# Gate/up products of a hybrid decoder block with tokens on partitions, three groups of tiles by Strassen's seven block products, and weight splits by whole pages

## Chip, cores, metric

One core of one Trainium2 chip runs the whole block in one launch. The metric is the device time in microseconds, as the median of several runs; less is better. A profile of one further execution gives the trace.

## What is computed

One decoder layer on 256 tokens of width 1024, all in fp32: a mixer (eight block-sparse MoBA heads and four differential heads, merged by two gates, one output projection), then a feed-forward part of width 2816. The change is in the feed-forward, but for the splits of weights, which serve every product.

```python
D_MODEL = 1024; SEQ = 256
D_FF = -(-8 * D_MODEL // (3 * 256)) * 256        # 2816
def reference(x, ..., w_gate, w_up, w_down, norm_ffn_post_g):
    ...
        merged = (jax.nn.sigmoid(ga) * (ya @ w_branch_a[l])
                  + jax.nn.sigmoid(gb) * (yb @ w_branch_b[l]))
        x = x + rms_norm(merged @ w_out[l], norm_mix_post_g[l])
        h = rms_norm(x, norm_ffn_pre_g[l])
        f = (jax.nn.silu(h @ w_gate[l]) * (h @ w_up[l])) @ w_down[l]
        x = x + rms_norm(f, norm_ffn_post_g[l])
    return x
```

## The kernel before

**Products.** Each operand is split exactly into two float32r parts, hi + lo, and each fp32 product is three matmuls: hi by hi, hi by lo, lo by hi (`mm3`, L227 to L229). Weights come raw from HBM through one ring of `RB` = 7 tiles of 128x1024 (512 KB), in one fixed order, all from SP's queue (`load_raws`, L191): a load waits until the tile seven before it has been split. ScalarE copies the raw half of 128x512 to hi (L209, `whi`), VectorE takes raw minus hi as lo (L212, `wlo`); the hi and lo tiles are rings of `WB` = 5.

**Order.** The work is a list of slots, each about 12 products of N=256. `run` walks through it, and before each slot it issues the splits that the next four slots need. PE and SP keep that order; ScalarE's, VectorE's and GpSimd's queues are ordered by the framework's scheduler, but for two stretches written by hand.

**Input projection and merge.** `group_T` makes q and k with columns on partitions, 4 banks `acc` of 512 columns each; VectorE takes a bank out by L446 (q). After the attention, `ab_slots` makes both branches; their products with the gates are added on GpSimd (L694, `mg`) and split into `mTh`, `mTl`, which `out_part` multiplies by w_out.

**Feed-forward.** The first four column tiles of gate and up (`NAT` = 4) have tokens on partitions: `nat`, with `h2h`/`h2l` stationary and 512 weight columns moving. Their result is turned by eight transposes (`nat_T`, L929). The other 18 tiles, f = 4 to 21, go through `gu_slots(f)`: a weight block of 128x128 is stationary, `h2h`/`h2l` of 128x256 moving, 8 k blocks x 3 x 2 (gate, up) = 48 matmuls of N=256 into one bank `s`. `ff_act` takes it out: times the column factor R2 (L882), silu, times up (L885), split into `fth`, `ftl`. R2 is made by `r2` (L909), products of ones by diagonal matrices `dg`. Behind tile f come the down terms of the tile before, `z_slots("d", ..)`: 15 matmuls, nine of N=512 and six of N=256, into three banks `acc` and one `pv`. The last four down terms are arranged by pieces (`z_tail`), and then come the norm, the residual and the output.

```python
    for f in range(NAT, NFF):
        slots += gu_slots(f)
        if f == NAT:
            slots[-2]["post"] = [nat_T]
        for i in downs(f):
            slots += z_slots("d", i, f_of, NFF - 1)
```

Of the kernel before, what the change touches and what calls it, by code (L numbers as in the profile page):

```python
# [64 lines left out]
def tile_hybrid_block(  # L65
# [37 lines left out]
    raws, gran, halves, extra, place = [], {}, [], [], {}  # L103

    def raw_of(w, r0, nr, c0, ncol):
        raws.append(dict(view=w[0, r0:r0 + nr * P, c0:c0 + ncol].rearrange("(a p) c -> p a c", p=P),
                         a=nr, c=ncol, uses=0, tile=None))
        return raws[-1]
# [897 lines left out]
```

## Time and profile before

| | |
|---|---|
| runs, us | 385.74, 385.76, 386.1; median 385.76 |
| span of the profiled execution, us | 383.0 |
| granted TensorE clock, mean | 0.995 |
| PE / VectorE / ScalarE / GpSimd busy, us | 375.3 / 270.9 / 221.6 / 40.2 |
| moved by DMA | 67.72 MB, mean 177 GB/s |

The profiled execution has no time of its own beside its span: the span runs from its first to its last instruction, and the device time of the runs has the launch and the end around it. PE is TensorE's matmul row, PEld its weight loads, DVE is VectorE, ACT ScalarE, POOL GpSimd, SP the queue that issues the loads. Busy times of PE overlap, since a matmul is still draining when the next one starts; what a matmul costs in a stream is read from start to start. A wait is shown as idle time before an instruction, with the instruction or load that released it.

### The profile page before, as it was taken

The numbers are of one execution on the slowest core, as the hardware profiler recorded it, in microseconds if no ns is written. First come the engines' busy times: TensorE is split into PE (matmuls) and PEld (weight loads), VectorE is DVE, ScalarE is ACT, GpSimd is POOL, SyncE is SP. The second block draws the span as 40 slices with busy tenths as digits, with TensorE's granted clock in tenths as the row PEclk, the third lists the DMA queues.
The fourth block names the chain that finished last, engine by engine and source line by source line (L and its number), as shares of the span: only waits on it lengthen the run. The fifth ranks groups of instructions, "written<-read, shape, count | busy, mean of one in ns | idle before, by whom it ended". The sixth has DMA issues, their size and how long they took to land.

```text
span 383.0 us, 7077 instructions
## 1 busy us (share of the span) xinstructions
PE 375.3 (98%) x2648; PEld 349.3 (91%) x2648; DVE 270.9 (71%) x596; ACT 221.6 (58%) x492; POOL 40.2 (11%) x59
## 2 busy tenths in 40 slices
PE   8999999999999999999999999999999999999993
PEld 5799989999999999998888998999999999999983
DVE  3799887989978769798768755655656566567524
ACT  4965675778565866555578544545445454456321
POOL 0199400000001002122100000000000000000000
PEclk9999999999999999999999999999999999999997
DMA  7989656263555436487118872755729274563003
GB/s 211 377 267 357 178 162 173 67 193 104 186 164 165 166 111 221 167 273 213 61 56 272 256 236 71 265 158 174 251 86 307 75 273 134 196 222 110 2 0 111
DMA packets 43813, 67.72 MB, mean 177 GB/s; under 512 B 2801, under 2 KB 27394, under 8 KB 43778
## 3 DMA queue, kind: packets, MB, share of 16 engines
q1 hardware_dynamic: 43778, 67.26, 53.8%
q8 instruction: 21, 0.34, 0.4%
q14 instruction: 14, 0.11, 0.1%
HBM read 66.20 MB, written 1.05 MB: 176 GB/s over the span
## 4 chain that ended last, share of the span: by engine, by line
PE 93%; DVE 2%; issue 2%; DMA 1%; SPq 0%; ACT 0%; POOLq 0%; POOL 0%; DVEq 0%; ACTq 0%
PE acc L227 14%; PE acc L229 13%; PE acc L228 13%; PE s L229 12%; PE s L228 12%; PE s L227 12%; PE acc L506 5%; PE pv L228 2%; PE pv L229 2%; PE pv L227 2%; DVE wlo L212 1%; DMA wraw<-in_w_in_dram 1%; PE t L228 1%; PE t L229 1%; PE t L227 1%
## 5 line engine op out<-in xcount | busy, mean ns | idle before, releaser
L212 DVE TENSOR_TENSOR wlo<-wraw,whi 128x512 fp32r<-128x512 f32 x234 | 157.7, 712 | 51.3 <-ACT whi L209 50.9
L209 ACT ACTIVATE whi<-wraw 128x512 fp32r<-128x512 f32 x233 | 133.9, 624 | 89.8 <-issue 42.1
L229 PE MATMUL s<-h2h,wlo 128*128 128x256 f32 x288 | 81.0, 281 | 0.0
L227 PE MATMUL s<-h2h,whi 128*128 128x256 f32 x288 | 80.9, 281 | 0.0
L228 PE MATMUL s<-h2l,whi 128*128 128x256 f32 x288 | 80.9, 281 | 0.0
L227 PE MATMUL acc<-hTh,whi 128*128 128x256 f32 x256 | 73.1, 286 | 0.4 <-DVE q L446 0.4
L229 PE MATMUL acc<-hTh,wlo 128*128 128x256 f32 x256 | 71.8, 281 | 0.0
L228 PE MATMUL acc<-hTl,whi 128*128 128x256 f32 x256 | 71.8, 281 | 0.0
L228 PEld LDWEIGHTS s<-h2l,whi 128*128 128x128 f32 x288 | 54.4, 189 | 0.0
L227 PEld LDWEIGHTS s<-h2h,whi 128*128 128x128 f32 x288 | 54.4, 189 | 0.0
L229 PEld LDWEIGHTS s<-h2h,wlo 128*128 128x128 f32 x288 | 54.2, 188 | 0.0
L227 PEld LDWEIGHTS acc<-hTh,whi 128*128 128x128 f32 x256 | 48.3, 189 | 0.7 <-DVE q L446 0.6
L228 PEld LDWEIGHTS acc<-hTl,whi 128*128 128x128 f32 x256 | 48.3, 189 | 0.0
L229 PEld LDWEIGHTS acc<-hTh,wlo 128*128 128x128 f32 x256 | 48.2, 188 | 0.0
L227 PE MATMUL acc<-whi,fth 128*128 128x512 f32 (+1 forms) x80 | 29.2, 365 | 0.0
L229 PE MATMUL acc<-whi,ftl 128*128 128x512 f32 (+1 forms) x80 | 29.1, 364 | 0.0
L228 PE MATMUL acc<-wlo,fth 128*128 128x512 f32 (+1 forms) x80 | 29.0, 362 | 0.0
L772 POOL TENSOR_TENSOR rs_r<-rs_e,mhalf 128x1 f32<-128x1 f32 x4 | 2.2, 552 | 190.3 <-DVE rs_e L771 190.3
L882 DVE TENSOR_TENSOR gs<-s,R 128x256 f32<-128x256 f32 x18 | 7.7, 425 | 16.4 <-PE s L229 16.4
L551 ACT ACTIVATE e<-e,nmx 128x256 f32<-128x256 f32 (+1 forms) x32 | 14.3, 447 | 5.8 <-DVE nmx L548 5.4
L229 PEld LDWEIGHTS acc<-whi,ftl 128*128 128x128 f32 x80 | 15.0, 188 | 2.5
L228 PEld LDWEIGHTS acc<-wlo,fth 128*128 128x128 f32 x80 | 15.0, 188 | 2.5
(253 smaller groups left out, 644.9 us busy)
## 6 DMA issues: line engine op xcount, KB each, us to landing
wraw<-in_w_in_dram SPq DMA_DIRECT2D x37, 512.0 KB, 4.8
wraw<-in_w_gate_dram SPq DMA_DIRECT2D x22, 512.0 KB, 4.6
wraw<-in_w_up_dram SPq DMA_DIRECT2D x22, 512.0 KB, 4.6
wraw<-in_w_down_dram SPq DMA_DIRECT2D x22, 512.0 KB, 4.6
wraw<-in_w_out_dram SPq DMA_DIRECT2D x8, 512.0 KB, 3.9
wraw<-in_w_branch_a_dram SPq DMA_DIRECT2D x4, 512.0 KB, 4.4
wraw<-in_w_branch_b_dram SPq DMA_DIRECT2D x4, 512.0 KB, 3.5
wraw<-in_w_in_dram SPq DMA_DIRECT2D x6, 256.0 KB, 4.4
```

Of the source, the lines that this page charges most:

```text
L209: nc.scalar.activation(hi, src, AF.Copy)
L212: nc.vector.tensor_tensor(lo, src, hi.bitcast(F32), op=OP.subtract)
L227: nc.tensor.matmul(dst, lh, rh, start=start, stop=False)
L228: nc.tensor.matmul(dst, lh, rl, start=False, stop=False)
L229: nc.tensor.matmul(dst, ll, rh, start=False, stop=stop)
L506: nc.tensor.matmul(acc[t], l[:, k, ts_], r, start=k == 0 and n == 0, stop=k == KT - 1 and n == 2)
L551: nc.scalar.activation(e[:, m, 0:n], e[:, m, 0:n], AF.Exp, bias=nmx[:, m:m + 1], scale=-1.0, accum_out=sm[:, m:m + 1])
L772: nc.gpsimd.tensor_tensor(r[:, 0:1], e, mhalf, op=OP.pow)
L882: nc.vector.tensor_tensor(gs, gp_, R2, op=OP.mult)
```

## The change

The 18 column tiles are taken in six units. **R** units (tiles 4-5, 10-11, 16-17) make two tiles as `nat` does: tokens stationary, 256 gate and 256 up columns side by side moving (N=512), one bank per token tile. **W** units (tiles 6-9, 12-15, 18-21) make four tiles as a 2x2 by 2x2 block product: rows are the two token tiles, the inner halves are k 0-3 and k 4-7, columns are gate (512) and up (512). Strassen's form in Winograd's order needs seven block products of 4 k instead of eight: 21, 11, T2, T1, T3, 22, T4, in two banks a and b of tag `s`. The sums of weight blocks T1 to T4 are made by VectorE (L268, eight instructions of 128x1024 per unit), the sums of activations once (`s_step`, L993, L998); the results are put together by q1 to q7 (L1026 to L1050): copies of banks by ScalarE (s1, s2, v5), sums by VectorE. f0 and f1, or `fr` of an R unit, are then transposed (`f_T`, L968) for the down terms: 44 transposes in all, and R2 with `r2` and `dg` is gone, since silu takes a factor by partition. Block weights lie in twelve raw "pages" besides the ring of seven; a page is loaded again when its last reader has been issued (`release`). T1 overwrites 12, T4 overwrites 21.

Splits go by whole pages of 128x1024 (L184 on ScalarE, L187 on VectorE) in place of two halves, but for the first projection group, z 4 to 7, gn, the first un page and the last four down tiles. `mg` is added on VectorE (L778). The number of bytes loaded stays.

```diff
+UNITS = [("R", 4), ("W", 6), ("R", 10), ("W", 12), ("R", 16), ("W", 18)]
...
+    def granule(n):
         g = gran[n]
         if g["hi"] is None:
             if n in place:
                 g["hi"], g["lo"] = place[n]()
             else:
-                hi = wpool.tile([P, 1024], F32R, tag="hi", name="whi")
-                lo = wpool.tile([P, 1024], F32R, tag="lo", name="wlo")
-                g["hi"], g["lo"] = [[t[:, 0:512], t[:, 512:1024]] for t in (hi, lo)]
-        r, view = g["src"][h]
-        src = view(r["tile"])
-        hi, lo = [t[h].rearrange("p (a c) -> p a c", a=g["a"]) for t in (g["hi"], g["lo"])]
-        if len(src.shape) == 2:
-            hi, lo = hi[:, 0, :], lo[:, 0, :]
+                g["hi"] = wpool.tile([P, 1024], F32R, tag="hi", name="whi")
+                g["lo"] = wpool.tile([P, 1024], F32R, tag="lo", name="wlo")
+        return g
...
+    def split_part(n, c, copy=None):
+        g = granule(n)
+        src, hi, lo = [t[:, c] for t in (g["raw"]["flat"], g["hi"], g["lo"])]
         if copy is None:
             nc.scalar.activation(hi, src, AF.Copy)
         else:
             copy(hi, src)
         nc.vector.tensor_tensor(lo, src, hi.bitcast(F32), op=OP.subtract)
-        r["uses"] -= 1
-        load_raws()
+        release(g["raw"])
...
+    def release(*rs):
+        for r in rs:
+            r["uses"] -= 1
+            if not r["uses"] and r["home"] == "page":
+                free.append(r["page"])
+        load_raws()
...
+    def load_raw(r):
+        if r["home"] == "page":
+            r["page"] = free.pop(0)
+            t = page(r["page"], "wpage")
+        else:
+            t = wpool.tile([P, 1024], F32, tag="raw", name="wraw", bufs=RB)
+            raw_home.append(r)
+        r["flat"] = t
+        r["tile"] = t.rearrange("p (a c) -> p a c", a=r["a"])
+        cur["raw"] += 1
...
+    def job_add(dst, a, b):
+        use(a, b)
+        touch(dst)
+        def f():
+            nc.vector.tensor_tensor(dst["flat"], a["flat"], b["flat"], op=OP.add)
+            release(a, b)
+        add_job(f)
...
+    def early_sums(f):
+        def two(w, k0):
+            return [raw_of([(slice(0, 512), rows(w, (k0 + 2 * i) * P, 2, f * P, 512))], 2, "page") for i in range(2)]
+        b = wsum[f] = {"11": two(w_gate, 0), "12": two(w_up, 0), "21": two(w_gate, 4), "22": two(w_up, 4)}
+        for n in ("T3", "T2"):
+            b[n] = [raw_of([], 2, "page") for i in range(2)]
+        b["T1"], b["T4"] = b["12"], b["21"]
+        return [lambda d=d, x=x, y=y, i=i: job_add(b[d][i], b[x][i], b[y][i])
+                for d, x, y in (("T3", "12", "22"), ("T1", "11", "12"), ("T2", "11", "T3")) for i in range(2)]
...
+            b = wsum[f0]
+            sp = {n: [lambda n=n, i=i: job_split((n, f0, i), b[n][i]) for i in range(2)]
+                  for n in ("11", "21", "22", "T1", "T2", "T3", "T4")}
+            t4 = [lambda i=i: job_add(b["T4"][i], b["T2"][i], b["21"][i]) for i in range(2)]
+            todo = sp["21"] + sp["11"] + ds[0:1] + t4[0:1] + ds[1:2] + t4[1:2]
+            for n in ("T2", "T1", "T3", "22", "T4"):
+                todo += sp[n]
+        for f in todo:
+            f()
...
-            nc.gpsimd.tensor_tensor(mg, pr[:, 0, :], pr[:, 1, :], op=OP.add)
...
+            nc.vector.tensor_tensor(mg, pr[:, 0, :], pr[:, 1, :], op=OP.add)
+            split(mg, *[m[:, c % 4, :] for m in mT[c // 4]])
...
+    def f_T(fv, f0, n, t, tag="t"):
+        def pe():
+            b = ps(tag)
+            for j in range(n):
...
+            split(b[:, 0:n * P], h, l)
...
+    def s_step(n):
+        full = [r["flat"].rearrange("p (k q) -> p k q", k=4) for r in sjobs[0:2]]
+        sf = [r["flat"].rearrange("p (r k q) -> p r k q", r=2, k=4) for r in sjobs[2:4]]
+        a = [[full[kh][:, :, t * P:(t + 1) * P] for kh in range(2)] for t in range(NT)]
+        r1, r2, r3, r4 = [sf[r // 2][:, r % 2, :, :] for r in range(4)]
+        if n < 2:
+            nc.vector.tensor_tensor(full[n], h2h[:, 4 * n:4 * n + 4, :].bitcast(F32),
+                                    h2l[:, 4 * n:4 * n + 4, :].bitcast(F32), op=OP.add)
+        elif n < 6:
+            d, x, y, op = [(r1, a[1][0], a[1][1], OP.subtract), (r2, r1, a[0][0], OP.subtract),
+                           (r3, a[0][0], a[1][0], OP.subtract), (r4, a[0][1], r2, OP.add)][n - 2]
+            nc.vector.tensor_tensor(d, x, y, op=op)
+        elif n < 8:
+            split(sjobs[n - 4]["flat"], *[Sp[2 * v + n - 6].rearrange("p r k q -> p (r k q)") for v in range(2)])
+        elif n == 8:
+            release(*sjobs)
...
+    def block(bank, a, n, f0, kp, start, stop):
+        w = W((n, f0, kp))
+        for j in range(2):
+            k = 2 * kp + j
+            mm3(bank, a(k), [v[:, j, :] for v in w], start=start and k == 0, stop=stop and k == 3,
+                skip_group_check=True)
...
+        def q1():
+            s1 = work.tile([P, 512], F32, tag="ph0", name="s1", bufs=1)
+            nc.scalar.activation(s1, st["a"], AF.Copy)
+            g = st["g0"] = work.tile([P, 512], F32, tag="e", name="g0", bufs=4)
+            nc.vector.tensor_tensor(g, st["b"], s1, op=OP.add)
+            nc.scalar.activation(g, g, AF.Silu, scale=rs2[:, 0:1])
+        def q6():
+            st["s2"] = work.tile([P, 512], F32, tag="ph0", name="s2", bufs=1)
+            nc.scalar.activation(st["s2"], st["a"], AF.Copy)
+        def q5():
+            st["v5"] = work.tile([P, 512], F32, tag="pl0", name="v5", bufs=1)
+            nc.scalar.activation(st["v5"], st["b"], AF.Copy)
+        def q7():
+            nc.vector.tensor_tensor(st["v5"], st["v5"], st["a"], op=OP.subtract)
+        def q3():
+            u = st["f0"] = work.tile([P, 512], F32, tag="e", name="f0", bufs=4)
+            nc.vector.tensor_tensor(u, st["b"], st["s2"], op=OP.subtract)
+            nc.vector.tensor_tensor(u, u, st["g0"], op=OP.mult)
+        def q4():
+            g = st["f1"] = work.tile([P, 512], F32, tag="e", name="f1", bufs=4)
+            nc.scalar.activation(g, st["a"], AF.Silu, scale=rs2[:, 1:2])
+            nc.vector.tensor_tensor(g, g, st["v5"], op=OP.mult)
+        head = slots_of("21", "b", A(0, 1), True, True, lambda: None)
+        body = slots_of("11", "a", A(0, 0), True, True, q1), [
+            s for x in (("T2", "a", R_(1), False, True, q6), ("T1", "b", R_(0), True, True, q5),
+                        ("T3", "a", R_(2), False, True, q7), ("22", "b", R_(3), False, True, q3),
+                        ("T4", "a", A(1, 1), False, True, q4)) for s in slots_of(*x)]
+        body[1].append(f_T(lambda: st["f0"], f0, 4, 0))
+        return head, body[0], body[1], [f_T(lambda: st["f1"], f0, 4, 1)]
...
+    def unit_R(f0):
+        st = []
+        def pe(kc, t):
+            if not st:
+                st.extend([dict(b=ps("s")), dict(b=ps("s"))])
+            w = W(("r", f0, kc))
+            for j in range(2):
+                k = 2 * kc + j
+                mm3(st[t]["b"], [v[:, k, t * P:(t + 1) * P] for v in (h2h, h2l)], [v[:, j, :] for v in w],
                     start=k == 0, stop=k == KT - 1)
-        sl = [dict(pe=lambda s=s, h=h: pe(s, h), need=[(("gu"[s], f), h)]) for s in range(2) for h in range(2)]
-        sl[3]["post"] = [lambda: ff_act(f, bank[0][:, 0:S], bank[0][:, S:2 * S])]
-        return sl
-    def r2():
-        b = ps("s")
-        for t in range(NT):
-            nc.tensor.matmul(b[:, t * P:(t + 1) * P], ones, dgs[t], start=True, stop=True)
-        nc.vector.tensor_copy(R2, b[:, 0:S])
...
+        def done(t):
+            g = st[t]["f"] = work.tile([P, 512], F32, tag="e", name="fr", bufs=4)[:, 0:256]
+            nc.scalar.activation(g, st[t]["b"][:, 0:256], AF.Silu, scale=rs2[:, t:t + 1])
+            nc.vector.tensor_tensor(g, st[t]["b"][:, 256:512], g, op=OP.mult)
+        sl = [dict(pe=lambda kc=kc, t=t: pe(kc, t), need=[(("r", f0, kc), 0)],
+                   post=[lambda t=t: done(t)] if kc == 3 else []) for kc in range(4) for t in range(NT)]
+        return sl[0:2], sl[2:4], sl[4:8], [f_T(lambda t=t: st[t]["f"], f0, 2, t) for t in range(NT)]
...
-        slots += gu_slots(f)
...
+    left = [f_T(lambda t=t: fgs[t], 0, 4, t, "pv" if t else "t") for t in range(NT)]
+    for i, (kind, f0) in enumerate(UNITS):
+        a, b, c, nxt = unit_W(f0) if kind == "W" else unit_R(f0)
+        zs = [s for f in units_before(i) for s in z_slots("d", f, f_of, NFF - 1)]
+        if i == len(UNITS) - 1:
+            slots += a + left + b + zs[0:2] + c + zs[2:4] + nxt
+        else:
+            slots += a + left + b + zs + c
+        left = nxt
```

**VectorE in the feed-forward.** Before, one column tile's rows in VectorE's queue (`gs` and `fv` are `ff_act`):

```order
L882 TENSOR_TENSOR gs<-s,R_2753 128x256
L212 TENSOR_TENSOR wlo<-wraw,whi 128x512 x2
L885 TENSOR_TENSOR fv<-s,gs 128x256
L234 TENSOR_TENSOR ftl<-fv,fth 128x256
L212 TENSOR_TENSOR wlo<-wraw,whi 128x512 x4
```

Now, in unit W6, from T1's first split on; tiles are numbered. wpage_2587 and wpage_2656 hold T1; wpage_3090 is a sum for W12, its inputs wpage_3063 and wpage_3078 are loaded, as is wpage_3106; 3102 to 3117 are T3, 3134 and 3145 block 22, 3157 and 3167 T4; s_3027 is bank a:

```order
L187 TENSOR_TENSOR wlo_3075<-wpage_2587,whi_3074 128x1024 [waits PE_49,Activation_49]
L187 TENSOR_TENSOR wlo_3087<-wpage_2656,whi_3086 128x1024 [waits Activation_49]
L268 TENSOR_TENSOR wpage_3090<-wpage_3063,wpage_3078 128x1024 [waits DMAHW7_49,DMAHW0_49,DVE_49]
L187 TENSOR_TENSOR wlo_3103<-wpage_2591,whi_3102 128x1024 [waits Activation_49]
L187 TENSOR_TENSOR wlo_3117<-wpage_2677,whi_3116 128x1024 [waits Activation_49]
L187 TENSOR_TENSOR wlo_3134<-wpage_2589,whi_3133 128x1024 [waits PE_49,Activation_49]
L187 TENSOR_TENSOR wlo_3145<-wpage_2675,whi_3144 128x1024 [waits Activation_49]
L268 TENSOR_TENSOR wpage_2985<-wpage_3106,wpage_2985 128x1024 [waits DMAHW2_49]
L187 TENSOR_TENSOR wlo_3157<-wpage_2802,whi_3156 128x1024 [waits PE_49,Activation_49]
L187 TENSOR_TENSOR wlo_3167<-wpage_2804,whi_3166 128x1024 [waits Activation_49]
L1040 TENSOR_TENSOR v5_3154<-v5_3154,s_3027 128x512 [waits PE_49]
L187 TENSOR_TENSOR wlo_3184<-wraw_2837,whi_3183 128x1024 [waits Activation_49]
```

What was a repeat of splits and one evacuation is now a queue with two sums for the next unit, each waiting for loads, ahead of splits that this unit needs and of L1040, which frees bank a.

SP's queue of those loads in the same place (the pages of W12's blocks 12, 22 and 11, between down tiles):

```order
L165 DMA wpage_2985<-in_w_up_dram 128x2x512 [waits DMAHW4_49,DVE_49]
L165 DMA wpage_2998<-in_w_up_dram 128x2x512 [waits DMAHW5_49,DVE_49]
L165 DMA wraw_3051<-in_w_down_dram 128x1024 [waits DMAHW6_49]
L165 DMA wpage_3063<-in_w_up_dram 128x2x512 [waits DMAHW7_49,DVE_49]
L165 DMA wpage_3078<-in_w_up_dram 128x2x512 [waits DMAHW0_49,DVE_49]
L165 DMA wraw_3091<-in_w_down_dram 128x1024 [waits DMAHW1_49]
L165 DMA wpage_3106<-in_w_gate_dram 128x2x512 [waits DMAHW2_49,DVE_49]
```

Each page waits for a release by VectorE; before, only the ring of seven stood there.

**PE at the end of W6.** T4's products (whi_3156, whi_3166; a row that repeats left out), then the transposes of f0, then the next R unit:

```order
L216 MATMUL s_3027<-whi_3156,h2h_2009 128x512 [waits DVE_49,Activation_49]
L217 MATMUL s_3027<-wlo_3157,h2h_2009 128x512
L218 MATMUL s_3027<-whi_3156,h2l_2010 128x512
L216 MATMUL s_3027<-whi_3166,h2h_2009 128x512 [waits Activation_49]
L217 MATMUL s_3027<-wlo_3167,h2h_2009 128x512
L218 MATMUL s_3027<-whi_3166,h2l_2010 128x512
L968 MATMUL t_3225<-ident_101,f0_3201 128x128 [waits DVE_49,PE_49]
L968 MATMUL t_3225<-ident_101,f0_3201 128x128 x3
L216 MATMUL s_3234<-whi_3183,h2h_2009 128x512 [waits Activation_49]
```

T4 waits for VectorE (bank a) and the transposes for f0; before, a tile's products were followed by the down terms of an earlier tile.

**VectorE at the q evacuation.** acc_303 to acc_332 are the four banks of q, before (rows of lambda, 128x1, left out):

```order
L212 TENSOR_TENSOR wlo_555<-wraw_280,whi_554 128x512 [waits DMAHW4_49,PE_49,Activation_49]
L446 TENSOR_TENSOR q_466<-acc_303,R1_143 128x256 [waits PE_49]
L446 TENSOR_TENSOR q_472<-acc_304,R1_143 128x256 [waits PE_49]
L212 TENSOR_TENSOR wlo_555<-wraw_280,whi_554 128x512 [waits Activation_49]
L234 TENSOR_TENSOR ql_469<-q_466,qh_468 128x256 [waits Activation_49]
L234 TENSOR_TENSOR ql_475<-q_472,qh_474 128x256 [waits Activation_49]
L446 TENSOR_TENSOR q_494<-acc_331,R1_143 128x256 [waits DVE_49,PE_49]
L446 TENSOR_TENSOR q_500<-acc_332,R1_143 128x256 [waits DVE_49,PE_49]
L212 TENSOR_TENSOR wlo_601<-wraw_301,whi_600 128x512 [waits DMAHW3_49,Activation_49]
```

and now (acc_307 to acc_336):

```order
L528 TENSOR_TENSOR q_462<-acc_307,R1_143 128x256 [waits PE_49]
L187 TENSOR_TENSOR wlo_545<-wraw_286,whi_544 128x1024 [waits DMAHW4_49,Activation_49]
L223 TENSOR_TENSOR q_464<-q_462,q_464 128x256 [waits Activation_49]
L528 TENSOR_TENSOR q_467<-acc_308,R1_143 128x256 [waits PE_49]
L528 TENSOR_TENSOR q_488<-acc_335,R1_143 128x256 [waits DVE_49,PE_49]
L187 TENSOR_TENSOR wlo_589<-wraw_305,whi_588 128x1024 [waits DMAHW3_49,PE_49,Activation_49]
L223 TENSOR_TENSOR q_469<-q_467,q_469 128x256 [waits Activation_49]
L223 TENSOR_TENSOR q_490<-q_488,q_490 128x256 [waits Activation_49]
L528 TENSOR_TENSOR q_493<-acc_336,R1_143 128x256 [waits DVE_49]
```

The fourth bank, acc_336, came behind one half split, and comes now behind two splits of whole pages.

## Rows read from the trace of the kernel before

**Rows 1.** The page's part 1: busy us (share of the span) xinstructions, by engine.
```profile
span 383.0 us, 7077 instructions
PE 375.3 (98%) x2648; PEld 349.3 (91%) x2648; DVE 270.9 (71%) x596; ACT 221.6 (58%) x492; POOL 40.2 (11%) x59
```

**Rows 2.** The page's part 4: the chain that ended last, shares by engine.
```profile
PE 93%; DVE 2%; issue 2%; DMA 1%; SPq 0%; ACT 0%; POOLq 0%; POOL 0%; DVEq 0%; ACTq 0%
```

**Rows 3.** Windows: span, its length, busy us of engines, PEclk, DMA share, GB/s.
```profile
20.00:40.00 20.00, 19.56 (x163) 19.19 (x163) 18.95 (x36) 11.88 (x24) 19.20 (x26) 1.00 0.89 300
80.00:100.00 20.00, 20.00 (x162) 19.57 (x161) 19.03 (x51) 15.06 (x40) 0.00 (x0) 1.00 0.43 127
217.00:364.00 147.00, 147.00 (x1097) 140.53 (x1095) 89.18 (x161) 73.64 (x143) 0.00 (x0) 1.00 0.52 174
```

**Rows 4.** Timeline of PE around 33 us: start us, us, engine, line, idle and releaser.
```profile
32.61 0.28 PE L229 MATMUL acc<-hTh,wlo 128*128 128x256 f32 x1
33.34 0.39 PE L227 MATMUL acc<-hTh,whi 128*128 128x256 f32 x1 [0.44 <-DVE q L446]
```

**Rows 5.** Timeline of PE, feed-forward: down terms, then a gate/up tile, first products.
```profile
252.74 0.39 PE L227 MATMUL acc<-whi,fth 128*128 128x512 f32 x1
...
253.19 0.39 PE L229 MATMUL acc<-whi,ftl 128*128 128x512 f32 x1
...
255.50 0.28 PE L227 MATMUL s<-h2h,whi 128*128 128x256 f32 x1
...
261.20 0.39 PE L227 MATMUL acc<-whi,fth 128*128 128x512 f32 x1
```

**Rows 6.** Timeline of PE, un products of two token tiles, r2, next un.
```profile
203.73 0.39 PE L227 MATMUL t<-whi,h2h 128*128 128x512 f32 x1
...
206.30 0.39 PE L229 MATMUL pv<-whi,h2l 128*128 128x512 f32 x1
206.53 0.61 PE L909 MATMUL s<-dg,ones 128*128 128x128 f32 x4
206.89 0.48 PE L227 MATMUL t<-whi,h2h 128*128 128x512 f32 x1
```

**Rows 7.** Timeline of PE, the transposes of line 929.
```profile
216.85 0.60 PE L929 MATMUL t<-ident,fgs 128*128 128x128 f32 x4
217.29 0.60 PE L929 MATMUL pv<-ident,fgs 128*128 128x128 f32 x4
```

**Rows 8.** Groups of VectorE instructions, 217 to 364 us: busy us, mean ns, idle before.
```profile
L212 DVE TENSOR_TENSOR wlo<-wraw,whi 128x512 fp32r<-128x512 f32 x101 | 65.4, 688 | 32.6 <-ACT whi L209 32.6
L882 DVE TENSOR_TENSOR gs<-s,R 128x256 f32<-128x256 f32 x18 | 7.7, 425 | 16.4 <-PE s L229 16.4
```

**Rows 9.** Timeline of VectorE: two in one row (x2) follow without a gap.
```profile
32.87 0.74 DVE L446 TENSOR_TENSOR q<-acc,R 128x256 f32<-128x256 f32 x2
...
290.30 1.29 DVE L212 TENSOR_TENSOR wlo<-wraw,whi 128x512 fp32r<-128x512 f32 x2 [0.34 <-ACT whi L209]
```

**Rows 10.** Groups of ScalarE (128x1024), and the tile mg (ns min/median/max).
```profile
L334 ACT ACTIVATE scr<-xt 128x1024 bf16<-128x1024 f32 x2 | 2.1, 1058 | 0.0
...
L694 POOL TENSOR_TENSOR mg<-pr x8: 1056/1060/1123, 146.9 to 175.2; 128x256 f32<-128x256 f32 x8
```

**Rows 11.** DMA issues: KB each, median us to landing; page, 170-182, 300-320 us.
```profile
wraw<-in_w_up_dram SPq DMA_DIRECT2D x22, 512.0 KB, 4.6
wraw<-in_w_branch_b_dram SPq DMA_DIRECT2D x4, 512.0 KB, 3.5
...
wraw<-in_w_up_dram SPq DMA_DIRECT2D x3, 512.0 KB, 3.7
...
wraw<-in_w_up_dram SPq DMA_DIRECT2D x2, 512.0 KB, 5.0
```

More of the change, by code (lines that the diff above doesn't have):

```diff
@@ L94, in tile_hybrid_block, with page @@
     psum = ctx.enter_context(tc.tile_pool(name="psum", bufs=1, space=PSUM))
+    def page(i, name, dt=F32):
+        return const.tile([P, 1024], dt, tag=f"g{i}", name=name)
     def ps(tag):
         return psum.tile([P, 512], F32, tag=tag, bufs={"acc": 4, "s": 2}.get(tag, 1), name=tag)
[L103 to L108, printed above, removed]
@@ new lines, in tile_hybrid_block, with raw_of, rows, raw1 @@
+    raw_order, raw_home, free = [], [], []
+    cur = dict(raw=0, job=0, extra=0)
+    def raw_of(views, a, home="raw"):
+        return dict(views=views, a=a, uses=0, home=home, there=False)
+    def rows(w, r0, nr, c0, ncol):
+        return w[0, r0:r0 + nr * P, c0:c0 + ncol].rearrange("(a p) c -> p a c", p=P)
+    def raw1(w, r0, nr, c0, ncol):
+        return raw_of([(slice(0, ncol), rows(w, r0, nr, c0, ncol))], nr)
+    def touch(r):
+        if not r["there"]:
+            r["there"] = True
+            raw_order.append(r)
@@ L195, in split_half @@
+            if r["home"] == "page":
+                if not free:
+                    break
+            elif len(raw_home) >= RB and raw_home[-RB]["uses"] > 0:
+                break
+            load_raw(r)
+            for c, v in r["views"]:
+                nc.sync.dma_start(r["tile"][:, :, c], v)
+    def granule(n):
         g = gran[n]
@@ L669, in tile_hybrid_block @@
     gp1 = post_gain(norm_mix_post_g)
-    mTh = const.tile([P, KT, S], F32R, tag="bias", name="mTh")
-    mTl = const.tile([P, KT, S], F32R, tag="vhl", name="mTl")
+    mT = [[page((0, 1, 2, 7)[2 * v + i], "mT", F32R).rearrange("p (k q) -> p k q", k=4) for v in range(2)]
+          for i in range(2)]
+    free.extend([8, 9])
     side = ["s", "s", "t", "pv"]
     def sig(c):
-        nc.scalar.activation(gate[:, c, :, :], gate[:, c, :, :], AF.Sigmoid)
+        nc.scalar.activation(gate[c], gate[c], AF.Sigmoid)
     def ab_slots(c):
@@ new lines, in block, with unit_W, bank, slots_of @@
+    def block(bank, a, n, f0, kp, start, stop):
[4 more added lines that the diff above has]
+                skip_group_check=True)
+    def unit_W(f0):
+        st = {}
+        def bank(n):
+            if n not in st:
+                st[n] = ps("s")
+            return st[n]
+        def slots_of(n, bk, a, start, stop, post):
+            return [dict(pe=lambda kp=kp: block(bank(bk), a, n, f0, kp, start, stop), need=[((n, f0, kp), 0)],
+                         post=[post] if kp else []) for kp in range(2)]
+        def q1():
[27 more added lines that the diff above has]
+        return head, body[0], body[1], [f_T(lambda: st["f1"], f0, 4, 1)]
```

322 lines of the change are left out of this document (147 added, 175 removed).

## The prediction

> **What bounds the kernel now.** I read the busy shares first [rows 1]: TensorE is busy 98% of the span, VectorE 71%, ScalarE 58%. The chain that ended last agrees: 93% of it is PE [rows 2]. Then the windows [rows 3], because a share is an average over stages: from 80 to 100 us and through the feed-forward, 217 to 364, PE is busy to the last hundredth, and from 20 to 40 us for 19.56 of 20; the granted clock is 1.00 in all three. VectorE differs by stage: 18.95 and 19.03 of 20 us in the early stretches, 89.18 of 147 in the feed-forward. So a product less is time won, one for one, as long as VectorE and the loads keep up, and the feed-forward, where the change is made, has 58 us of idle VectorE to spend. Short PE stops exist: one of 0.44 us at 33.34, released by VectorE's evacuation L446 [rows 4]. A difference of under 0.2% (0.77 us) is taken for no change.
>
> **Prices on TensorE, from starts to starts.** A gate/up column tile runs from 255.50 to 261.20, 5.70 us for 48 products of N=256 (0.119 each); the down terms of one tile, 252.74 to 255.50, take 2.76 [rows 5]. The form that the change uses, tokens stationary and 512 weight columns moving, stands in the trace already, in the un products: 203.73 to 206.53 holds 12, 0.233 each; the r2 broadcast behind them takes 0.36 [rows 6]. Four 128x128 transposes take 0.44 [rows 7], 0.11 each.
>
> **1. Products.** Eighteen column tiles cost 18 x 5.70 = 102.6 us. After: an R unit has 48 products of N=512, a W unit 7 blocks x 4 k x 3 = 84 (without Strassen 96). 3 x 48 + 3 x 84 = 396, x 0.233 = 92.4. That is -10.2: nearly all from the W units (22.8 to 19.6 us each), since N=512 per column is hardly cheaper than N=256. At the price of the down terms (252.74 to 253.19 holds two, 0.225) it would be -13.5, the far end; I take the un rows, because they are this very form.
> The Trainium skill has a table for this (TensorE: Matmul & The Clock Gate, section Back-to-back issue gap): 262 cycles for N=256, 518 for N=512. By it the 864 products would cost 94.3 us and the 396 85.5, a gain of only 8.9 (estimate from that page). The trace has both forms 8 to 9% slower than the table, N=256 the more so, and the trace decides.
>
> **2. Transposes.** The results now have tokens on partitions and must be turned: 44 transposes for 8, 36 more. At 0.11 that is +3.9; none is hidden, PE does them. r2 goes: -0.36. PE's own sum: -10.2 + 3.9 - 0.36 = **-6.7 us**.
>
> **3. VectorE's load.** A weight split of 128x512 has a duration of 688 ns in the feed-forward, one of 128x256 some 425 [rows 8]; back to back, two splits end in 1.29 us, so the second starts 0.60 after the first, and two 128x256 in 0.74, so 0.33 [rows 9]. The line through both gives 0.60 + 2 x 0.27 = 1.14 us for a whole page of 128x1024 (estimate; its duration 1.22). A page split saves 0.06 against two halves; beside a busy PE that is worth nothing. ScalarE's 128x1024 takes 1.06 [rows 10]; it has room.
> From 217 to 364 us VectorE had 89 us. After: 103 instructions of a page (72 splits of blocks, R rows and down tiles, 24 weight sums, 3 of un, 4 of the activation sums), 39 of 512 and 12 of 256 make 103 x 1.14 + 39 x 0.60 + 12 x 0.33 = 145 us. They aren't spread evenly. In W6's own stage VectorE's queue holds 15 page splits, 3 sums for W12, 5 evacuations of 512 and 2 splits of 256: 18 x 1.14 + 5 x 0.60 + 2 x 0.33 = 24.2 us. PE's time there is 84 x 0.233 + 2 x 2.76 + 8 x 0.11 = 26.0. That leaves 1.8 us for every wait in that queue, and the scheduler has put sums there that wait for loads.
>
> **4. The waits in W6 and W12** (0 = first product of block 21; W12's rows have the same pattern). Five hi/lo buffers are in turn, so T2's first split follows the end of block 21 (12 x 0.233 = 2.8) and its hi (1.06): 3.9. Then two page splits, a sum, two fT splits, g0 and T1's first split: 3.9 + 4 x 1.14 + 2 x 0.33 + 0.60 + 0.08 (its end) = 9.8. Only now is the raw page under T1's first half free, and SP issues the last page of the second sum for W12. Its landing: the un pages, 2 KB to a row like these, took 3.7 us [rows 11]; so 13.5. The sum stands ahead of T3's splits, so VectorE idles for 2 us. Sum and T3's first split end at 15.9, the page under it is loaded, landing 19.6; the third sum waits for that and ends at 20.7. Two T4 splits and L1040 (v5 -= bank a) end at 23.7. T4's products need that bank and PE is there at 22.7 (7 blocks and downs, less T4, plus the four transposes): **stop of 1.0**. VectorE goes on with r0, u, r1, f0: 23.6 + 2 x 1.14 + 2 x 0.60 = 27.1, end 27.2. PE wants f0 for its transposes at 23.7 + 2.8 = 26.5: **stop of 0.7**. So 1.7 for each of W6 and W12, +3.4. W18 has no following sums in its queue, and an R unit has some 14 pages, 16 us, beside 48 x 0.233 + 4 x 2.76 = 22 us of PE: nothing there. Bounds by the landing, which enters twice per unit: the shortest row, 3.5 (branch_b), gives 1.3 a unit, +2.6; the median 4.6 gives 3.5, +7.0 [rows 11].
>
> **5. q evacuation at 33 us.** Before, the four L446 come in pairs, with one half split between (the order shown with the change). Now the fourth comes behind two whole pages: the PE stop of 0.44 grows by about one page in place of a half and its neighbour, +0.65 (0 to +0.9).
>
> **6. Rest.** The merge add leaves POOL (1.06 us each) for VectorE (0.33): its chain to mTh shortens by 0.6, against whole-page splits that it now may queue behind; PE showed no stop there, so 0 (-0.3 to +1.5). SP's loads are the same bytes. The tail keeps its halves: 0.
>
> **Sum.** -6.7 + 3.4 + 0.65 = -2.65, against the profiled execution's span of 383.0: 380.35. The runs' median, 385.76, lies 2.76 above that span, for what is outside it; I carry that over: **383.1 us**.
>
> **Rivals.**
> A. *The queue covers the waits.* If the page split is nearer 1.05 (two halves in one, one pass) VectorE gains 0.09 on each of the 18 pages, 1.6 us, and the stop before T4 goes; that before f0 shrinks. For it: PE ran without a stop from 80 to 100 us, where VectorE was busy for 19.03 of 20 [rows 3]. Against: a wait for a load is not shortened by faster arithmetic. Time: -6.7 + 0 to 1.3: 379.0 to 380.5.
> B. *The loads inside VectorE's queue decide, the other side.* If pages land at 4.6, as the median load does, the two units stop for 7.0 us: -6.7 + 7.0 + 0.65 = +0.95, 386.7; at 5.0, as two loads did at 300 to 320 us [rows 11], 2 x 4.3 = 8.6: 388.3. It decides from a landing of 4.4, where the stops reach 6.05 and the gain is gone. For it: the raw ring still loads in the same SP queue. Against: the pages are issued about 2 us apart, when little else is in flight.
> C. *VectorE is itself the bound in W units.* If no two instructions overlap, a page costs its whole 1.22, a 512 0.69: 18 x 1.22 + 5 x 0.69 + 2 x 0.425 = 26.3 us against 26.0 of PE. Between the first late page and f0 lie 8 pages and 3 evacuations, +0.9 a unit, and 0.5 in W18: +2.3 on the sum, 385.4. Against it: rows 9, where starts are 0.09 closer than durations.
> The Trainium skill's rule of that kind is in VectorE: DVE Perf Modes, section on the TRN2 errata: an fp32 two-tensor add takes (N + 151)/0.96 ns, and SBUF's latency is paid between instructions, once for each tile. It gives 1.22 us for a page (estimate), what case C has; the trace agrees on the duration (688 ns for its 691) but not that it is paid in full.
>
> **Chances.** Forecast, with stops of 1.3 to 2.5 a unit (382 to 384.9): 0.40. A (below 382): 0.20. C, or landings of 4.2 to 4.4: 0.16, no change that can be told. B, with the attention's +1.5 as its far end: 0.24. So faster 0.60, same 0.16, slower 0.24. The range leaves out a tenth at either end: 379.2, A with little left of the stops, and 388.0, B just short of a landing of 5.0. The forecast's own range is 381.5 to 384.9.
>
> **What would show it.** PE's product time in the W units at 0.233 a product and PE's total busy time down by about 6.7 less the stops; a gap before T4's first product released by L1040 and one before the transposes L968 released by L1045, in W6 and W12 and not in W18; VectorE idle before L268 released by a DMA; L187's page split at 1.22 long; a gap of over 1 us near 33 us. Wrong would be: stops in the R units or at W18, a page split over 1.3, PE gaps on ScalarE's copies, or products at other than 0.233.

## The result: slower by 3.2%

The changed kernel takes 398.05 us (median of 4 runs, 397.57 to 399.47), the kernel before 385.75 in the same comparison: a ratio of 1.032, interval 1.0301 to 1.034. The forecast was 383.1, in a range of 379.2 to 388.0.

The page of the changed kernel: busy shares, the chain by engine, and VectorE's page splits.

```profile
span 397.7 us, 6046 instructions
PE 375.9 (95%) x2212; PEld 326.8 (82%) x2212; DVE 311.1 (78%) x523; ACT 234.2 (59%) x402; POOL 34.0 (9%) x51
...
PE 82%; DVE 7%; DMA 6%; issue 2%; ACT 2%; SPq 1%; DVEq 0%; POOLq 0%; ACTq 0%
...
L187 DVE TENSOR_TENSOR wlo<-wpage,whi 128x1024 fp32r<-128x1024 f32 x42 | 50.6, 1223 | 18.9 <-ACT whi L184 18.8
```

PE's share fell from 98% to 95% and its part of the chain from 93% to 82% [rows 1, 2]: PE now waits. VectorE's part rose from 2 to 7%, the loads' from 1 to 6%. A page split lasts 1.22 us, as estimated.

What PE waited for (engine, line waited for: us in total, times, the longest):

```profile
PE t L968 <- DVE fT L223: 7.6, 3, 2.5
PE acc L216 <- DVE q L528: 1.6, 1, 1.6
PE s L216 <- DVE v L1040: 1.6, 1, 1.6
PE s L216 <- ACT whi L184: 1.1, 1, 1.1
PE s L432 <- DMA xt<-in_x_dram: 1.1, 1, 1.1
...
PE t L968 <- DVE f L1045: 0.9, 2, 0.4
```

One line is larger than all others: three waits of 2.5 us by the transposes L968 for VectorE's split of `fT`. The window in which unit W6 begins, in the columns of [rows 3]:

```profile
240.00:260.00 20.00, 17.48 (x78) 14.13 (x77) 12.89 (x13) 11.70 (x15) 0.00 (x0) 0.91 0.41 129
```

PE misses 2.5 us of it, and the granted clock is 0.91: two losses in one place, where [rows 3] had 147.00 of 147 and 1.00. The timeline of that place, where R4's results are turned behind W6's first block (PE, ACT and DVE rows; start, duration, operation, idle before):

```profile
241.73 0.38 PE L968 MATMUL t<-ident,fr 128*128 128x128 f32 x2
241.93 1.06 ACT L184 ACTIVATE whi<-wpage 128x1024 fp32r<-128x1024 f32 x1 [0.34 <-PE s L218]
242.89 0.36 ACT L222 ACTIVATE fT<-t 128x256 fp32r<-128x256 f32 x1
243.02 1.23 DVE L187 TENSOR_TENSOR wlo<-wpage,whi 128x1024 fp32r<-128x1024 f32 x1 [0.17 <-ACT whi L184]
244.16 0.42 DVE L223 TENSOR_TENSOR fT<-t,fT 128x256 fp32r<-128x256 f32 x1
...
244.63 0.44 PE L968 MATMUL t<-ident,fr 128*128 128x128 f32 x2 [2.52 <-DVE fT L223]
...
244.83 0.48 PE L216 MATMUL s<-whi,h2h 128*128 128x512 f32 x1
...
246.58 0.63 PE L216 MATMUL s<-whi,h2h 128*128 128x512 f32 x1
...
247.01 0.63 PE L217 MATMUL s<-wlo,h2h 128*128 128x512 f32 x1
...
249.14 0.51 PE L216 MATMUL acc<-whi,fT 128*128 128x512 f32 x1
```

Read it downwards. PE transposes R4's first token tile into bank `t` at 241.73. ScalarE should copy it, but the hi of a whole page, begun at 241.93, goes first; the copy runs at 242.89. VectorE then has the lo of that page (243.02, 1.23 us) ahead of the rest of the split (244.16). Only at 244.63 may PE transpose the second token tile, because `f_T` takes the one bank `t` again; the two groups of transposes of tiles 0 to 3 took two banks, `t` and `pv` [rows 7]. Block 11 follows at 244.83 and its later products start 0.43 us apart, in place of 0.233, at a granted clock of 0.50 (246.2 to 249.1 us): the 1.2 GHz level. The two stretches by themselves:

```profile
241.73:244.63 2.90, 0.38 (x3) 0.14 (x1) 2.73 (x4) 1.33 (x2) 0.00 (x0) 1.00 0.39 160
244.83:249.14 4.31, 4.31 (x14) 3.37 (x14) 2.44 (x3) 1.44 (x2) 0.00 (x0) 0.63 0.00 0
```

PE was busy for 0.38 of 2.90 us; in the 4.31 us of the next twelve products the granted clock is 0.63 on average. At the head of W12 and of W18 (297 and 352 us) the stops are as long, 2.52 us, and the slow products begin as soon as PE goes on: the twelve of block 11 take 4.43 and 4.22 us.

The two stops that the prediction worked out are there too. VectorE in W6:

```profile
256.96 1.23 DVE L268 TENSOR_TENSOR wpage<-wpage 128x1024 f32<-128x1024 f32 x1 [2.37 <-DMA wpage<-in_w_up_dram]
258.10 4.62 DVE L187 TENSOR_TENSOR wlo<-wpage,whi 128x1024 fp32r<-128x1024 f32 x4
263.44 1.23 DVE L268 TENSOR_TENSOR wpage<-wpage 128x1024 f32<-128x1024 f32 x1 [0.71 <-DMA wpage<-in_w_gate_dram]
264.58 2.35 DVE L187 TENSOR_TENSOR wlo<-wpage,whi 128x1024 fp32r<-128x1024 f32 x2
266.85 0.68 DVE L1040 TENSOR_TENSOR v<-v,s 128x512 f32<-128x512 f32 x1
```

and PE, before T4 and before f0's transposes:

```profile
265.72 0.40 PE L218 MATMUL s<-whi,S 128*128 128x512 f32 x1
267.68 0.47 PE L216 MATMUL s<-whi,h2h 128*128 128x512 f32 x1 [1.56 <-DVE v L1040]
...
270.32 0.40 PE L218 MATMUL s<-whi,h2l 128*128 128x512 f32 x1
271.15 0.63 PE L968 MATMUL t<-ident,f 128*128 128x128 f32 x4 [0.43 <-DVE f L1045]
```

VectorE sat idle for 2.37 us before the second sum (forecast: 2) and 0.71 before the third, both released by loads; L1040 ended behind two T4 splits, and PE waited 1.56 us for it and 0.43 for f0 (forecast: 1.0 and 0.7).

The q evacuation, and a new stop in the attention:

```profile
34.44 0.28 PE L218 MATMUL acc<-hTh,wlo 128*128 128x256 f32 x1
36.35 0.39 PE L216 MATMUL acc<-hTh,whi 128*128 128x256 f32 x1 [1.63 <-DVE q L528]
...
94.81 0.41 PE L656 MATMUL pv<-ident,e 128*128 128x128 f32 x2 [0.59 <-DVE ya L223]
```

The gap at 34 us is 1.91 us from start to start where it was 0.73 [rows 4].

### The profile page after: what moved, and what is told of

Its sections match the earlier page's. It is cut to its first block, busy times and chain, and to the rows that moved or that the text cites. A ratio compares the mean times of both kernels' runs of the same rounds, so it can differ in the third digit from the quotient of the medians.

```text
span 397.7 us, 6046 instructions
## 1 busy us (share of the span) xinstructions
PE 375.9 (95%) x2212; PEld 326.8 (82%) x2212; DVE 311.1 (78%) x523; ACT 234.2 (59%) x402; POOL 34.0 (9%) x51
## 4 chain that ended last, share of the span: by engine, by line
PE 82%; DVE 7%; DMA 6%; issue 2%; ACT 2%; SPq 1%; DVEq 0%; POOLq 0%; ACTq 0%
PE acc L216 13%; PE acc L217 13%; PE acc L218 13%; PE s L216 9%; PE s L217 8%; PE s L218 8%; PE acc L589 5%; DVE wlo L187 4%; DMA wpage<-in_w_up_dram 2%; DMA wpage<-in_w_gate_dram 2%; PE pv L217 2%; PE pv L218 2%; PE pv L216 2%; ACT whi L184 2%; DMA xt<-in_x_dram 1%
## 5 line engine op out<-in xcount | busy, mean ns | idle before, releaser
L187 DVE TENSOR_TENSOR wlo<-wraw,whi 128x1024 fp32r<-128x1024 f32 (+1 forms) x105 | 114.9, 1106 | 22.9 <-ACT whi L184 20.5
L184 ACT ACTIVATE whi<-wraw 128x1024 fp32r<-128x1024 f32 (+1 forms) x104 | 98.6, 962 | 57.5 <-PE acc L217 23.4
L187 DVE TENSOR_TENSOR wlo<-wpage,whi 128x1024 fp32r<-128x1024 f32 x42 | 50.6, 1223 | 18.9 <-ACT whi L184 18.8
L184 ACT ACTIVATE whi<-wpage 128x1024 fp32r<-128x1024 f32 x42 | 44.1, 1060 | 32.4 <-PE pv L218 18.7
L216 PE MATMUL s<-whi,h2h 128*128 128x512 f32 x92 | 39.4, 428 | 2.7 <-DVE v L1040 1.6
L217 PE MATMUL s<-wlo,h2h 128*128 128x512 f32 x92 | 38.2, 416 | 0.0
L218 PE MATMUL s<-whi,h2l 128*128 128x512 f32 x92 | 38.0, 413 | 0.0
L268 DVE TENSOR_TENSOR wpage<-wpage 128x1024 f32<-128x1024 f32 x24 | 29.1, 1219 | 5.8 <-DMA wpage<-in_w_up_dram 4.3
L216 PE MATMUL acc<-whi,fT 128*128 128x512 f32 (+1 forms) x80 | 29.2, 365 | 0.0
L218 PE MATMUL acc<-whi,fT 128*128 128x512 f32 (+1 forms) x80 | 29.1, 364 | 0.0
L217 PE MATMUL acc<-wlo,fT 128*128 128x512 f32 (+1 forms) x80 | 29.1, 364 | 0.0
```

The source lines that it names most:

```text
L184: nc.scalar.activation(hi, src, AF.Copy)
L187: nc.vector.tensor_tensor(lo, src, hi.bitcast(F32), op=OP.subtract)
L216: nc.tensor.matmul(dst, lh, rh, start=start, stop=False, **kw)
L217: nc.tensor.matmul(dst, lh, rl, start=False, stop=False, **kw)
L218: nc.tensor.matmul(dst, ll, rh, start=False, stop=stop, **kw)
L268: nc.vector.tensor_tensor(dst["flat"], a["flat"], b["flat"], op=OP.add)
```

## The experiments

All were compared with the kernel before on the same chip; its median was 385.6 to 386.0. The edits are given in short and not as the code has them.

**One bank for both token tiles** (e1_one_bank)

```diff
-f_T(t=0): 2 transposes into t; split 128x256; f_T(t=1): the same bank again
+f_T2: 4 transposes into the two halves of t; one split 128x512
```

> Edit: the transposes of an R unit's two token tiles go into the two halves of one bank t and are taken out by one split of 128x512, so no transpose waits for the bank. Theory B (bank): the 2.52 us stop before the second pair of transposes L968 behind each of the three R units, and the stretch of slow products behind it (12 products of block 11 in 4.2 to 4.4 us and not 2.8), are all of what makes the change slower than before: 3 x (2.5 + 1.5) = 12 us less than the changed kernel's 398.05, so 385.5 to 386.5, and the granted clock 1.00 from 240 to 260 us. Rival V (VectorE's load): the 145 us of VectorE work in the feed-forward is the bound and the time comes back as other stops in the W units: 392 to 396.

386.37 us, ratio to before 1.0015 (1.0002 to 1.0028): 11.7 us less than the change as it was. Its windows and the place itself:

```profile
240.00:260.00 20.00, 20.00 (x96) 16.46 (x95) 16.83 (x16) 15.18 (x18) 0.00 (x0) 1.00 0.65 220
260.00:280.00 20.00, 18.33 (x90) 14.67 (x89) 18.64 (x20) 9.84 (x11) 0.00 (x0) 1.00 0.64 219
...
241.09 0.60 PE L985 MATMUL t<-ident,fr 128*128 128x128 f32 x4
241.44 0.48 PE L216 MATMUL s<-whi,h2h 128*128 128x512 f32 x1
```

The four transposes take 0.35 us and block 11 follows at once; the clock is 1.00. What is left in the feed-forward is the stops before T4 and f0: 1.23 and 0.44 us in W6 (the second window), 1.39 and 0.43 in W12. VectorE's work is the same, but for one split of 128x512 in place of two of 128x256: rival V is out.

**The single bank, with products between** (e2_apart)

```diff
-slots += a + left + b + zs + c
+slots += a + left[0:1] + b + left[1:] + zs + c      # behind R units
```

> Edit: the bank stays single, but the transposes of an R unit's second token tile stand behind block 11 of the next W unit, 12 products of 2.8 us later. Theory B: the drain of the bank took 2.5 us and now has 2.8 us of products to hide behind; the stops fall to under 0.5 us each and the clock stays at 1.00: 386 to 387.5. Rival V: VectorE is as late as before, and the stop only moves to block 11 or to the down terms: 394 to 398.

387.02 us, 1.0034 (1.0019 to 1.0048). The two pairs of transposes behind R4:

```profile
243.69 0.38 PE L968 MATMUL t<-ident,fr 128*128 128x128 f32 x2
...
246.72 0.38 PE L968 MATMUL t<-ident,fr 128*128 128x128 f32 x2
```

The bank was as late, since VectorE's split of the first pair ended at 246.55, 2.86 us behind the start of the transposes (2.85 in the changed kernel). But PE had 2.9 us of products to do meanwhile, and the second pair starts without a wait. Two different edits that share only the wait take nearly the same time away: the wait is the cause.

**Idle products in the stop** (e11_fill)

```diff
+for i in range(10): matmul(bank a, h2h, h2h)     # between the two pairs of transposes; never read
```

> Edit: the changed kernel with its single bank and its stop, but between the two pairs of transposes behind each R unit PE gets ten idle products of N=512 (2.33 us), written into the bank that block 11 starts afresh afterwards; nothing reads them. They stand where PE stood still. Theory K (the slow products behind the stop are the price of PE standing still, apart from the stop itself): the granted clock stays at 1.00 from 240 to 260 us, block 11 takes 2.8 us and not 4.2 to 4.4, and 3 x 1.5 = 4.5 us less than 398.05: 393 to 394.5; the other 7.6 us stay, now as idle products. Rival (the slow products come from something else in that stretch, loads or VectorE): block 11 stays at 4.2 us or more, 397.5 to 398.5.

394.77 us, 1.0224 (1.0206 to 1.0242), just above what was expected: 3.3 us less by the medians, 4.8 by the two profiled spans (392.9 and 397.7), although PE does 7 us of useless work. PE's rows and a window:

```profile
241.68 2.57 PE L1061 MATMUL s<-h2h 128*128 128x512 f32 x10
244.46 0.44 PE L968 MATMUL t<-ident,fr 128*128 128x128 f32 x2 [0.20 <-DVE fT L223]
244.65 0.48 PE L216 MATMUL s<-whi,h2h 128*128 128x512 f32 x1
...
247.53 0.39 PE L216 MATMUL acc<-whi,fT 128*128 128x512 f32 x1
...
240.00:260.00 20.00, 19.80 (x94) 16.00 (x93) 14.52 (x15) 13.14 (x17) 0.00 (x0) 1.00 0.43 141
```

The twelve products of block 11 take 2.88 us where they took 4.31, at a clock of 1.00, with VectorE as busy as before (2.74 of 2.91 us between the pairs, 2.73 of 2.90 before). So the slow products are the price of PE having stood still. From the second pair of transposes to the first down product the three units take 1.44, 1.55 and 1.49 us less, 4.5 in all, besides the stop. Why the medians show 3.3 and not 4.5 is open; the profiled execution of the changed kernel, in which all three stretches are slow, was its slowest.

**Halves in the input projection** (e3_p_halves)

```diff
-job_split(("p", g, kc), ..., (0, 1) if g == GROUPS[0] else None)
+job_split(("p", g, kc), ..., (0, 1))
```

> Edit: only the input projection's weight pages are split in halves of 128x512 again (the feed-forward as in the changed kernel). Theory G (whole pages make short evacuations wait longer): the PE gap at 34 us falls from 1.91 to about 0.7 us and those at 92 to 95 us (0.5 and 1.2) go: -1.2 to -2.3, so 395.7 to 396.9. Rival: the gaps come from the loads or the order of the evacuations, not from the size of the split: 397.5 to 398.5.

395.79 us, 1.0266 (1.0206 to 1.0326), 2.3 less, the far end of what was expected, but the runs spread from 393.48 to 398.51, and the interval is as wide as the gain. The traces decide. The gap at 33 us:

```profile
33.34 0.28 PE L218 MATMUL acc<-hTh,wlo 128*128 128x256 f32 x1
34.13 0.38 PE L216 MATMUL acc<-hTh,whi 128*128 128x256 f32 x1 [0.50 <-DVE q L528]
```

0.79 us from start to start, about as before; the stops at 92 to 95 us are gone (PE 20.00 of 20 from 80 to 100 us). From the projection's first product to the attention's first score product PE takes 26.95 us in place of 28.32 (27.08 before the change), and from there to the merge's first product 96.43 in place of 97.82 (96.49 before): 1.4 us each. Whole pages cost here what they were not priced at: a short evacuation behind them waits longer.

**The sums out of the W units** (e4_late_sums)

```diff
-todo += d0, T3_0, d1, T3_1, d2, T1_0, d3, T1_1, r2, T2_0, r3, T2_1
+todo += d0, d1, d2, d3, r2, r3, T3_0, T3_1, T1_0, T1_1, T2_0, T2_1
```

> Edit: in the list of splits and sums the sums for the next W unit stand behind the R unit's own splits, so VectorE's queue in W6 and W12 holds none of them. Theory L (the prediction's, loads inside VectorE's queue): the stops before T4's first product released by L1040 (1.72 and 1.26 us in the changed kernel) go, -2.5, and those before f0's transposes (0.36 each) stay or go: 394.8 to 395.8. Rival: VectorE has no room for the six sums in the R unit's 22 us, and block 21 or 11 of the next W unit waits for its splits instead: 397.5 to 400.

395.39 us, 1.0251 (1.0205 to 1.0297), 2.7 less, give or take 1.8. The stops before T4 and f0 are gone, and a new one came, which the rival foresaw only in part: the next unit's first products wait for the R unit's bank, since its evacuation `fr` stands behind the six sums. The wait, and the stretches around the transposes at 295 us:

```profile
295.32:298.10 2.78, 0.27 (x3) 0.03 (x1) 2.57 (x3) 1.33 (x2) 0.00 (x0) 1.00 0.72 208
298.30:301.20 2.90, 2.90 (x15) 2.36 (x15) 0.54 (x2) 1.45 (x2) 0.00 (x0) 1.00 0.40 141
...
PE s L216 <- DVE fr L1072: 2.3, 2, 1.7
```

After this stop, as long as the others (2.52 us), the clock stayed at 1.00; so part of the 2.7 us, some 1.5, is a missing fall of the clock and not the edit's work. Such a stop makes the fall likely and not certain: in the profiles of the three kernels that have it (the changed one, e3_p_halves and this) seven of nine such stops were followed by one. It shows in the spread of the runs: here 393.75 us at a mean granted clock of 0.994, 398.17 at 0.982. What decides between the two is open.

**Putting them together** (e8_t0, e5_comb, e6_comb4)

```diff
+c: kc 2, 3 of token tile 0, then of token tile 1      # R unit's last slots, e8_t0
+a[0], f0's transposes, a[1], b, f1's transposes       # in the next R unit, e8_t0
+sums behind all splits (e5_comb); each four down tiles later (e6_comb4)
```

> Edits: one bank for both token tiles' transposes (as in e1_one_bank), halves in the input projection (as in e3_p_halves); besides, the last two steps of an R unit run token tile 0 to its end before token tile 1, and f0's transposes stand after the first slot of the next unit, f1's after the fourth. Sums stay inside the W units. From e1_one_bank's 386.37: -2.3 for the halves (e3_p_halves' part), -0.7 for f0's two stops, -0.2 for the bank freed late: 383.2, with the two stops before T4's first product still there (1.2 and 1.3 us). If the shorter queues only make VectorE fall behind elsewhere: 385 to 386.5.

> Edits: those of e8_t0, and the sums for the next W unit behind the R unit's own splits (as in e4_late_sums). Theory (stops are separate and add): -2.5 more than e8_t0, 380.7, PE without a stop over 0.3 us after 40 us. Rival (VectorE has no room for the six sums in an R unit): the stops come back before block 21 or 11 of W12 and W18, released by VectorE's evacuation of the R unit, as the 1.7 and 0.4 us in e4_late_sums did: 382 to 384.

> Edits: those of e8_t0, and each sum for the next W unit moved four down tiles later in the list of splits: two of the six stay in the W unit's queue, ahead of T1 and T3, the third, which ended last, comes behind T4. Theory L (the load of the page that is freed last makes the stop before T4): the T4 stops fall from 1.2 to under 0.5 and no stop appears in the R units: 380.5 to 382. Rival (any sum in the W unit is too much for VectorE there): as e8_t0, 383.

384.33 us, 0.9959 (0.9946 to 0.9972); 382.39, 0.9917 (0.9904 to 0.993); 382.03, 0.9897 (0.9883 to 0.9911). All are faster than the kernel before. e8_t0 still has two stops before T4 (1.6 and 0.6 us by the waits); e5_comb and e6_comb4 have none, so the sums, and the loads that they wait for, were what held T4 up. e5_comb's time is one that its rival gave, but the stops that the rival named, before block 21 or 11, are not there. The first two missed their numbers by 1.1 and 1.7 us, the third lies at the edge, for one reason, which is an edit of mine: f1's transposes now stood right ahead of the down terms, which wait for their split. PE in e6_comb4:

```profile
267.98 0.40 PE L218 MATMUL acc<-whi,fT 128*128 128x512 f32 x1
268.88 0.50 PE L216 MATMUL acc<-whi,fT 128*128 128x512 f32 x1 [0.50 <-ACT fT L222]
```

The second row starts 0.90 behind the first, where 0.23 is due. e8_t0 and e5_comb have the same gap, e5_comb a second one of 1.04 us behind it.

**f1's transposes one slot earlier** (e9_comb5)

```diff
-a[0], f0's transposes, a[1], b, f1's transposes
+a[0], f0's transposes, a[1], b[0], f1's transposes, b[1]
```

> Edits: those of e6_comb4, and in an R unit f1's transposes stand one slot earlier, between the two slots before the down terms. In e6_comb4 the down terms stopped twice for 0.44 us (ScalarE's copy of f1's transposes) and 0.05 us (VectorE's), behind both R units that follow a W unit. Theory (the drain of bank t needs about 2 us of products): both stops go, -1.0: 381.0. Rival (the copy stands behind a page split on ScalarE and VectorE that waits for its buffer, wherever the transposes are): 382.0, as e6_comb4.

379.10 us, 0.984 (0.9817 to 0.9864). Better than expected, because I had added up the waits and not read the starts: the four down tiles behind each of these transposes took 12.24 us in e6_comb4, from first to next start, and 10.98 here, so 2.5 us in two units and not 1.0. The feed-forward, from the first un product (the up half of tiles 0 to 3) to the last down product, and what PE still waited for:

```profile
203.69:371.85 168.16, 168.16 (x813) 139.16 (x811) 148.22 (x155) 104.71 (x127) 2.01 (x2) 1.00 0.50 178
...
PE s L433 <- DMA xt<-in_x_dram: 2.2, 1, 2.2
PE pv L390 <- DVE first L351: 1.0, 1, 1.0
PE acc L216 <- DVE q L529: 0.4, 1, 0.4
```

168.16 of 168.16, with VectorE busy for 148.22: PE never waited for it there.

**Halves in four units** (e10_halves)

```diff
+if n is a page of R4, W6, R10, W12: halves = (0, 1)
```

> Edits: those of e9_comb5, and the weight pages of units R4, W6, R10 and W12 (36 of them) are split in halves of 128x512 as before the change; down tiles and the last two units stay whole. Price of two halves 1.20 us on VectorE against 1.14: 36 x 0.06 = 2.2 us more of VectorE's time. If VectorE has slack in these units once the stops are gone: as e9_comb5 within 0.4 us. Rival (whole pages are what lets VectorE keep up in a W unit, with 24 us of work in 26): new stops in W6 and W12, +1 to +3 us.

378.89 us, 0.9824 (0.981 to 0.9839): the same. Whole pages bring nothing in the feed-forward once PE does not wait.

**No Strassen** (e7_all_r)

```diff
-UNITS = [("R", 4), ("W", 6), ("R", 10), ("W", 12), ("R", 16), ("W", 18)]
+UNITS = [("R", f) for f in range(4, 22, 2)]
```

> Edits: no Strassen at all, nine R units of two column tiles, one bank for both token tiles, halves in the input projection. It computes the same. 9 x 48 = 432 products in place of 396: at 0.233 each +8.4 us against a Strassen form without stops (380.7): 389; by PE's sum against the kernel before: -1.9 for the products, +3.9 for 36 transposes, -0.4 for r2: 387.4. So 387 to 389.5, and no stop of PE in the feed-forward, since VectorE has no sums. Rival (the W units give back in stops and sums what they save in products): 382 to 384, better than e5_comb.

390.65 us, 1.0126 (1.0112 to 1.014), above what was expected; it is 11.6 us more than e9_comb5, of which the 36 products are 8.4. The rest are starts that come some 0.2 us late at each of its unit borders, and one stop of 0.8 and one of 0.4 us, by its trace. The rival is out: three Strassen units are the whole gain. Tokens on partitions alone, with their transposes, lose 4.8 us to the kernel before, of which 1.6 were worked out as PE's sum; the others are stops that another order might remove, which no run shows.

## Why the prediction was wrong

1. **PE's sum, -6.7: right.** e9_comb5 and e10_halves, without a stop in the feed-forward, are 6.5 and 6.7 us faster than before; the feed-forward itself is 7.0 shorter (below). Inside, four transposes took 0.35 and not 0.44, and the products 0.233.
2. **"An R unit has some 14 pages, 16 us, beside ... 22 us of PE: nothing there": this step failed.** It weighed VectorE's work against PE's time. The R unit's results are turned at the head of the next W unit, in two pairs of transposes 0.14 us apart through a bank that exists once. The second pair waits for a drain (the copy and the split that take the results out of the bank) by two engines, each with a whole page ahead: three stops of 2.5 us, 7.6 in all. One of them stands in W18, which the prediction had named as a sign of being wrong. My list of W6's waits had "two fT splits" in VectorE's queue, priced them, and didn't ask whether PE needed the bank between them. The Trainium skill has the rule (Perfetto Trace Analysis, section Optimizing Tensor Performance): independent groups of matmuls should rotate through different PSUM banks, so that evacuating one overlaps the next. The trace agrees, with 2.52 us for a drain of 128x256.
3. **The clock was left out.** Every term counted a stop at its own length. 1.4 to 1.6 us of slow products came on top behind each of the three stops, 4.5 in all (e11_fill).
4. **The stops before T4 and f0, +3.4: right in kind and nearly in size.** W6 lost 1.56 and 0.43 us, W12 1.10 and 0.43 by the waits: 3.5. From start to start it is 4.2. Without the bank's stop ahead of them, in e1_one_bank, the waits are 1.67 and 1.82 a unit, where the forecast was 1.7. Only W12's first is put down to ScalarE's hi and not to L1040. The two pages that were to decide were issued at 252.21 and 259.35, and the sums that waited for them began at 256.96 and 263.44: 4.7 and 4.1 us, longer than the 3.7 taken.
5. **q evacuation, +0.65: too small.** It was 1.2 (1.91 for 0.73 from start to start), beyond the 0.9 that was the far end; e3_p_halves shows that the pages are the cause.
6. **The rest, 0 (to +1.5): right for the merge, 1.3 too little for the attention.** From the merge's first product to the first un product PE took 57.90 us before and 57.80 now. The attention ahead of it grew from 96.49 to 97.82, and e3_p_halves takes that back. I had taken PE's missing stops there for slack.
7. **VectorE's price, 1.14 a page: right.** Four splits took 4.62 us (258.10 above), 1.13 from start to start. The rule in the Trainium skill (VectorE: DVE Perf Modes, section on the TRN2 errata) gives 1.22 for one (estimate), which is its duration; paid one after another it would be 4.9. Rival C is out.

The sum after the fact goes by the two profiles, from start to start. The feed-forward, from the first un product to the last down product, before and in the changed kernel:

```profile
200.93:376.06 175.13, 175.13 (x1248) 164.71 (x1247) 106.35 (x192) 87.64 (x173) 0.55 (x1) 1.00 0.51 171
204.44:390.58 186.14, 175.03 (x812) 142.20 (x811) 148.96 (x158) 104.73 (x130) 2.00 (x2) 0.97 0.46 155
```

With the 168.16 of e9_comb5 that is -7.0 for the work and +18.0 for what stopped or slowed PE: 8.1 for the three stops at the bank (2.70 each beyond what is due), 4.5 for the slow products, 4.2 before T4 and f0, and 1.2 in other starts that come late. The q evacuation adds 1.2, the attention 1.3, the first 10 us 1.0: +14.5 in all, of the 14.7 between the two profiled spans. The medians are only 12.3 apart: the profiled execution of the changed kernel (399.47 us) is its slowest, and the span of 383.0 is 0.5 to 1.6 us shorter than every later one of the kernel before (383.5 to 384.6).

In the first 10 us PE waited 1.1 us for a load of x. The profiles of the changed family show such a wait of 0.7 to 2.3 us, except that of e11_fill; the one of before shows none. It differs between executions of one kernel: with 2.2 us of it e9_comb5's profiled execution took 381.04 us, its other three 378.85 to 379.28. SP issues the same loads in the same order there, so its cause stays open.

Rivals A and B both argued about loads and VectorE's speed. The largest part of the loss lay in neither.

## To carry to other kernels

When work on PE is moved to another form, list the PSUM banks of each step and ask, for every second use of a bank, what its drain stands behind on ScalarE and VectorE; a bank used twice within 0.2 us is a full round trip on PE, however little those engines have to do on average. Put products between the two uses, or both results into one bank, before judging the arithmetic: the same 396 products gave 398.05 us or, with halves in the input projection and the sums moved too, 379.1. Larger instructions on the draining engines lengthen such waits, as the q evacuation showed, and a stop of 2.5 us cost another 1.5 in products at the lower clock in seven cases of nine.
